# The exact rest of 30 weight slabs from an adding DMA in place of a VectorE subtraction

## The chip, the cores and the metric

The kernel runs on one core of a Trainium2 chip. The time is the device time of one execution in microseconds. Times are compared as medians over several runs.

## The reference

Two transformer-like blocks are applied to 512 tokens of width 1024 in float32. Every dense layer is a product of activations with a weight matrix of a size like 1024 x 5632 or 2816 x 1024.

```python
h = modulate(rmsnorm(x, norm1_g), shift1, scale1)        # shift, scale, gate: silu(c) @ ada_w + ada_b
u, v, val, gate = split(h @ w_in + b_in)                  # four parts of 512 columns
y_a = spatial_gating_mixer(gelu(u), gelu(v), ...)         # causal 128 x 128 mixing in chunks
y_b = conformer_conv_mixer(val, gate, ...)                # GLU, depthwise convolution of width 31, norm, silu
x = x + gate1 * (concat(rmsnorm(y_a), rmsnorm(y_b)) @ w_out)
g_ff, up_ff = split(modulate(rmsnorm(x, norm2_g), shift2, scale2) @ w_ffn_in)
x = x + gate2 * ((silu(g_ff) * up_ff) @ w_ffn_out)
...                                                       # then attention, pooling and two more FFNs
```

The change concerns the weights `w_in`, `w_out` and the first columns of `w_ffn_in`, all in the first block.

## The kernel before

TensorE multiplies in a rounded 32-bit type, float32r. To keep the accuracy of float32, each operand is split into a head and an exact rest: `wh` is the weight rounded to float32r, `wl` is the weight minus `wh`. An activation `H` is split in the same way into `hh` and `hl`. A product is then three matmuls, `wh*hh + wh*hl + wl*hh`. `Opd.mm3s` issues them in this order for each block k of 128 rows, into one PSUM accumulator, so `wl` of a slab is wanted by the third matmul of its group. `mm_tok` does the same with tokens as rows.

Weights come in slabs of 128 partitions x 1024 elements (0.5 MB). A slab of `w_in` for val, gate or u, or of `w_ffn_in`, has 8 blocks of 128 columns, which are runs of 512 bytes in memory; a slab for v has 2 blocks of 512 columns; a slab of `w_out` has 4 blocks of 256. The class `Weights` keeps a plan of all slabs in the order of their use (`plan`), loads one over SyncE's queue into a tile `raw` (`load`, line 309), and then `split` makes `wh` on ScalarE (a copy that rounds) and `wl` on VectorE (`raw - wh`). `W.look` says how many split slabs are to be ready ahead (4 here). The tiles `raw`, `wh`, `wl` and the tiles `adaw` of the conditioning weights share one pool of 37 buffers of 4 KB per partition, so a load can wait in SyncE's queue until a buffer comes free, and everything behind it in that queue waits too.

A scheduler at compile time sets the order of each engine's instructions and places the waits. In `split`, `tc.high_priority(offset=hp)` lets the slabs of `w_in` and `w_out` go ahead of other work (`HP` is 300 for them, 0 for the FFN). Up to line 828 the order on VectorE, ScalarE and TensorE is that of the program; after it the scheduler is free.

The order of the work around the change is this. The first four slabs (val and gate of c = 0 and 1) are multiplied while the conditioning is computed. Then come val and gate of c = 2 and 3 (four slabs), v (four), u (four), and the output projection `w_out` (eight). Between these products VectorE works off the depthwise convolution, one tap at a time (`tap`, `pump`). Of the taps of lag 17 or 23 and more (`ND`), ScalarE makes the scaled copy and GpSimd adds it (40 such additions on GpSimd). `ada_fetch` puts loads of `adaw` into the same SyncE queue. Then the first FFN starts: for each m a gate slab and an up slab, in two halves of 256 tokens for m = 0 to 2, and on all 512 tokens after that.

A flag `W.pool` could send a slab's subtraction to GpSimd. With `WP = 0` and `UP = 0` no slab is sent there.

Of the kernel before, what the change touches and what calls it, by code (L numbers as in the profile page):

```python
# [9 lines left out]
F32 = mybir.dt.float32  # L10
F32R = mybir.dt.float32r
AF = mybir.ActivationFunctionType
OP = mybir.AluOpType
# [7 lines left out]
FF = 2816  # L21
# [36 lines left out]
PP4 = 0  # L58
PP5 = 2
PP = (PP0, PP1, PP2, PP3, PP4, PP5)  # L60
WP = 0
UP = 0
PY = 4
PZ = 4
GNV = False
# [55 lines left out]
def body(ctx: ExitStack, tc: tile.TileContext, I: dict, out, dbg=None):  # L121
    nc = tc.nc
# [6 lines left out]
    V, G, SC, TE = (Ordered(tc, e) for e in (nc.vector, nc.gpsimd, nc.scalar, nc.tensor))  # L129
# [4 lines left out]
    def A(name, dt=F32):  # L134
        tag, bufs = TAGS.get(name, ("m", NB))
        return ar.tile([P, 2, S], dt, tag=tag, name=name, bufs=bufs)
# [22 lines left out]
    def act(o, i, f=AF.Identity, **kw):  # L159
        ins = SC.activation(o, i, f, **kw)  # L160
        if f in KEEPF and not SC.on:
            tc.keep_in_program_order(ins)
        return ins
# [120 lines left out]
    class Weights:  # L284


        def __init__(self, look):
            self.look, self.deep = look, 1
            self.specs, self.loaded, self.ready, self.done = [], [], [], 0
            self.pool = False  # L290
            self.hp = 0

        def plan(self, parts, kt, ncols):
            self.specs.append((parts, kt, ncols, self.pool, self.hp))

        def load(self):
            parts, kt, ncols, pool, hp = self.specs[self.done]
            n = kt * ncols

            def fl(t):  # L300
                return t.rearrange("p a c -> p (a c)")[:, :n]

            def v(t):
                return fl(t).rearrange("p (k m) -> p k m", k=kt)

            raw = ar.tile([P, 2, S], F32, tag="raw", name="raw", bufs=NR) if NR else A("raw")
            for (p0, p1, c0, c1, src, *ks) in parts:
                k0, k1 = ks or (0, kt)
                nc.sync.dma_start(v(raw)[p0:p1, k0:k1, c0:c1], src)
            self.done += 1  # L310

            def split():
                wh, wl = A("wh", F32R), A("wl", F32R)
                with tc.high_priority(offset=hp) if hp else nullcontext():
                    act(fl(wh), fl(raw), AF.Copy)
                    (G if pool else V).tensor_tensor(fl(wl), fl(raw), fl(wh).bitcast(F32), op=OP.subtract)
                self.ready.append((v(wh), v(wl), kt))
            self.loaded.append(split)

# [16 lines left out]
            return self.ready.pop(0)  # L336

    W = Weights(4)
    W.pool = True

    def rows_of(w, k0, kt, c0, n):
        return w[k0 * P:(k0 + kt) * P, c0:c0 + n].rearrange("(k p) m -> p k m", p=P)
# [1 line left out]
    def plan_cols(w, k0, kt, c0, n):  # L344
        W.plan([(0, P, 0, n, rows_of(w, k0, kt, c0, n))], kt, n)

    w_in = I["w_in"][0]
    for c in range(4):
        W.pool = c < WP
        W.hp = HP  # L350
        plan_cols(w_in, 0, 8, 1024 + c * P, P)
        plan_cols(w_in, 0, 8, 1536 + c * P, P)
# [5 lines left out]
        for g in range(4):  # L358
            plan_cols(I["w_out"][0], k0, 4, g * HS, HS)

    W.pool = False
    W.hp = 0

    def plan_ffn_tok(gate, up, down):
# [8 lines left out]
            for k0 in range(KT0, KF, 2):  # L373
                plan_cols(down, k0, 2, j * S, S)

    def plan_ffn(gate, up, down, pool=False):
        def gu(m):
            plan_cols(gate, 0, 8, m * P, P)
            plan_cols(up, 0, 8, m * P, P)

        def dn(m, k0, kts):
            for kt in kts:
                plan_cols(down, k0, kt, m * P, P)
                k0 += kt
        for m in range(KF0 + 1):
            W.pool = pool and m < 4
            gu(m)
        for m in range(KD - 1):
            dn(m, 0, (7, 7))
        for m in range(KF0 + 1, KF):  # L390
            gu(m)
        dn(KD - 1, 0, (7, 7))
        for m in range(KD):
            dn(m, KF0, (8,))

    plan_ffn(I["w_ffn_in"][0][:, :FF], I["w_ffn_in"][0][:, FF:], I["w_ffn_out"][0], UP)

    awi = I["attn_w_in_2"][0]
    FQ, FK, FV, FFG, NQ, KC, VC, KS, VS, KW, VW, NG = 0, 512, 1024, 1536, 1544, 2056, 2184, 2312, 2440, 2568, 2696, 2824
# [488 lines left out]
    for h in range(8):  # L888
        hp, e = divmod(h, 2)
# [399 lines left out]
    def K2(name):  # L1289
        return A(name, F32R), A(name, F32R)  # L1290
    ks, kw = K2("ks"), K2("kw")
# [489 lines left out]
```

## Time and profile before

| | |
|---|---|
| median of 3 runs | 1670.14 us (1670.02 to 1671.48) |
| profiled execution | 1667.07 us |
| its span, first to last instruction | 1665.3 us |
| TensorE busy | 1627.4 us |
| VectorE, ScalarE, GpSimd busy | 881.8, 681.8, 129.5 us |
| moved by DMA | 179.55 MB |
| mean granted clock of TensorE | 0.993 |

In the rows, PE is TensorE, DVE is VectorE, ACT is ScalarE, POOL is GpSimd, SPq is SyncE's queue. Most instructions bear the line of a helper, L113, so they are told apart by their tiles: `wl<-raw,wh` is the subtraction, `wh<-raw` the head. In a timeline a row can hold several like instructions (x2), and a bracket gives the engine's idle time before them and what ended it.

### The profile page before, as it was taken

What the parts mean: (1) busy time and instruction counts of PE and PEld (TensorE: products, weight loads), DVE (VectorE), ACT (ScalarE), POOL (GpSimd) and SP (SyncE); (2) the same over time, 40 slices, a digit from 0 to 9 for tenths busy, and PEclk for the clock granted to TensorE, in tenths of its full rate; (3) what the DMA queues carried; (4) which work ended last, traced back from release to release, by engine and by line L of the source; (5) the groups of instructions that cost most, each with busy time, mean ns of one, the idle gap of its engine ahead of it and who ended that gap; (6) DMA issues with size and microseconds to landing.
All of it is one profiled execution on the core that took longest, in us unless ns stands there. A gap on an engine that the chain in (4) does not pass through costs nothing.

```text
span 1665.3 us, 22096 instructions
## 1 busy us (share of the span) xinstructions
PE 1627.4 (98%) x8797; PEld 1358.9 (82%) x8797; DVE 881.8 (53%) x1645; ACT 681.8 (41%) x1232; POOL 129.5 (8%) x144
## 2 busy tenths in 40 slices
PE   7999899999999999999999999999999999999998
PEld 5776698887888998777778988888888998888886
DVE  5799585444333584678857344423257734432144
ACT  4585352222222364455658233213237823232232
POOL 0452000000000001100001000000013100000002
PEclk9999999999999999999999999999999999999999
DMA  9635435544531423311144232234134232232411
GB/s 306 179 111 193 152 112 175 154 149 133 153 101 54 120 57 90 90 26 52 39 107 124 61 111 61 95 114 144 59 102 114 77 89 77 83 121 93 121 64 51
DMA packets 245168, 179.55 MB, mean 108 GB/s; under 512 B 20688, under 2 KB 220224, under 8 KB 245064
## 3 DMA queue, kind: packets, MB, share of 16 engines
q1 hardware_dynamic: 240520, 176.99, 36.3%
q10 hardware_dynamic: 4544, 1.14, 0.4%
q8 instruction: 69, 1.13, 0.3%
q14 instruction: 35, 0.29, 0.1%
HBM read 175.99 MB, written 2.11 MB: 107 GB/s over the span
## 4 chain that ended last, share of the span: by engine, by line
PE 86%; DVE 3%; ACT 2%; issue 0%; DMA 0%; SPq 0%; DVEq 0%; ACTq 0%
PE mm L113 79%; PE ax L113 4%; PE st L113 3%; DVE pw L113 1%; ACT sq L113 0%; DMA raw<-in_w_out_dram 0%; ACT pw L113 0%; DVE XT L113 0%; DVE wl L113 0%; DVE sq L113 0%; ACT wh L113 0%; ACT H L113 0%; DVE pt L113 0%; DVE fk L113 0%; DVE mg L113 0%
## 5 line engine op out<-in xcount | busy, mean ns | idle before, releaser
L113 PE MATMUL mm<-H,wh 128*128 128x512 f32 (+1 forms) x3168 | 869.8, 361 | 9.2 <-ACT wh L113 3.4
L113 PEld LDWEIGHTS mm<-H,wh 128*128 128x128 f32 x3168 | 564.1, 189 | 104.5 <-issue 4.4
L113 PE MATMUL mm<-H,wl 128*128 128x512 f32 (+1 forms) x1584 | 567.7, 359 | 2.9 <-DVE wl L113 2.9
L113 DVE TENSOR_TENSOR wl<-raw,wh 128x1024 fp32r<-128x1024 f32 (+1 forms) x257 | 310.4, 1223 | 217.0 <-ACT wh L113 203.2
L113 PEld LDWEIGHTS mm<-H,wl 128*128 128x128 f32 x1584 | 299.3, 189 | 47.7 <-DVE wl L113 3.5
L113 ACT ACTIVATE wh<-raw 128x1024 fp32r<-128x1024 f32 (+1 forms) x257 | 262.5, 1041 | 127.3 <-PE mm L113 52.8
L113 PE MATMUL mm<-wh,hid 128*128 128x512 f32 x704 | 217.3, 389 | 0.0
L113 DVE TENSOR_TENSOR silu<-silu,mm 128x512 f32<-128x512 f32 (+1 forms) x77 | 47.0, 611 | 250.0 <-PE mm L113 243.5
L113 PEld LDWEIGHTS mm<-wh,hid 128*128 128x128 f32 x704 | 132.1, 188 | 27.1
L113 ACT ACTIVATE hid<-silu 128x512 fp32r<-128x512 f32 (+1 forms) x77 | 43.8, 569 | 242.5 <-DVE silu L113 234.9
L113 PE MATMUL mm<-wl,hid 128*128 128x512 f32 x352 | 137.3, 390 | 0.0
L113 PE MATMUL mm<-hid,wh 128*128 128x512 f32 (+1 forms) x464 | 116.4, 340 | 0.0
L113 PEld LDWEIGHTS mm<-hid,wh 128*128 128x128 f32 x464 | 80.3, 190 | 9.9 <-issue 0.4
L113 POOL TENSOR_TENSOR mg<-mg,gb 128x512 f32<-128x512 f32 x32 | 44.3, 1389 | 464.6 <-ACT sq L113 456.0
L113 ACT ACTIVATE silu<-silu 128x512 f32<-128x512 f32 (+1 forms) x52 | 29.3, 565 | 123.1 <-DVE silu L113 123.0
L113 PE MATMUL mm<-hid,wl 128*128 128x512 f32 (+1 forms) x232 | 79.1, 341 | 0.0
L113 PEld LDWEIGHTS mm<-wl,hid 128*128 128x128 f32 x352 | 66.1, 188 | 14.0 <-DVE wl L113 0.3
L113 DVE TENSOR_TENSOR silu<-mm,rsb 128x512 f32<-128x512 f32 (+1 forms) x52 | 31.6, 608 | 73.0 <-PE mm L113 72.5
L113 PE MATMUL mm<-wh,H 128*128 128x512 f32 (+2 forms) x256 | 67.0, 350 | 1.6 <-ACT wh L113 1.6
L113 DVE TENSOR_TENSOR hid<-silu,hid 128x512 fp32r<-128x512 f32 (+1 forms) x77 | 47.3, 614 | 37.4 <-ACT hid L113 37.3
L113 POOL TENSOR_TENSOR cv<-cv,tap 128x488 f32<-128x488 f32 (+12 forms) x40 | 52.5, 1348 | 88.2 <-ACT cv L113 71.2
L113 ACT ACTIVATE silu<-mm 128x512 f32<-128x512 f32 (+1 forms) x25 | 13.7, 546 | 108.7 <-PE mm L113 108.7
(271 smaller groups left out, 1624.7 us busy)
## 6 DMA issues: line engine op xcount, KB each, us to landing
adaw<-in_ada_w_dram SPq DMA_DIRECT2D x48, 512.0 KB
raw<-in_w_ffn_in_dram SPq DMA_DIRECT2D x44, 512.0 KB
raw<-in_ffn_w_gate_dram SPq DMA_DIRECT2D x44, 512.0 KB
raw<-in_ffn_w_up_dram SPq DMA_DIRECT2D x44, 512.0 KB
raw<-in_ffn_w_down_dram SPq DMA_DIRECT2D x44, 512.0 KB
raw<-in_w_in_dram SPq DMA_DIRECT2D x16, 512.0 KB
adaw<-in_ada_f_w_dram SPq DMA_DIRECT2D x16, 512.0 KB
raw<-in_attn_w_in_dram SPq DMA_DIRECT2D x16, 512.0 KB
```

Source lines behind the costliest of these rows:

```text
L113: ins = f(*a, **k)
```

## The change

A flag `dma` takes the place of `pool`. For a slab with the flag, ScalarE writes `-wh` into the tile `wl` (a second copy, with scale -1), and a DMA issued from GpSimd reads the weights once more from memory and adds them to that tile in SBUF: `wl = -wh + w`. VectorE does nothing for such a slab. Without the flag all stays as it was. The flag is set for val and gate of c = 2 and 3, and stays set for v, u and `w_out` (20 slabs); `UD = 5` sets it for gate and up of the first five m of the first FFN (10 slabs).

```diff
@@ -58,8 +58,7 @@
 PP4 = 0
 PP5 = 2
 PP = (PP0, PP1, PP2, PP3, PP4, PP5)
-WP = 0
-UP = 0
+UD = 5
 PY = 4
 PZ = 4
 GNV = False
@@ -287,14 +286,14 @@
         def __init__(self, look):
             self.look, self.deep = look, 1
             self.specs, self.loaded, self.ready, self.done = [], [], [], 0
-            self.pool = False
+            self.dma = False
             self.hp = 0
 
         def plan(self, parts, kt, ncols):
-            self.specs.append((parts, kt, ncols, self.pool, self.hp))
+            self.specs.append((parts, kt, ncols, self.dma, self.hp))
 
         def load(self):
-            parts, kt, ncols, pool, hp = self.specs[self.done]
+            parts, kt, ncols, dma, hp = self.specs[self.done]
             n = kt * ncols
 
             def fl(t):
@@ -313,7 +312,14 @@
                 wh, wl = A("wh", F32R), A("wl", F32R)
                 with tc.high_priority(offset=hp) if hp else nullcontext():
                     act(fl(wh), fl(raw), AF.Copy)
-                    (G if pool else V).tensor_tensor(fl(wl), fl(raw), fl(wh).bitcast(F32), op=OP.subtract)
+                    if dma:
+
+                        act(fl(wl), fl(wh).bitcast(F32), AF.Copy, scale=-1.0)
+                        for (p0, p1, c0, c1, src, *ks) in parts:
+                            k0, k1 = ks or (0, kt)
+                            nc.gpsimd.dma_start(v(wl)[p0:p1, k0:k1, c0:c1], src.bitcast(F32R), accum_op=OP.add)
+                    else:
+                        V.tensor_tensor(fl(wl), fl(raw), fl(wh).bitcast(F32), op=OP.subtract)
                 self.ready.append((v(wh), v(wl), kt))
             self.loaded.append(split)
 
@@ -336,7 +342,6 @@
             return self.ready.pop(0)
 
     W = Weights(4)
-    W.pool = True
 
     def rows_of(w, k0, kt, c0, n):
         return w[k0 * P:(k0 + kt) * P, c0:c0 + n].rearrange("(k p) m -> p k m", p=P)
@@ -346,7 +351,7 @@
 
     w_in = I["w_in"][0]
     for c in range(4):
-        W.pool = c < WP
+        W.dma = c >= 2
         W.hp = HP
         plan_cols(w_in, 0, 8, 1024 + c * P, P)
         plan_cols(w_in, 0, 8, 1536 + c * P, P)
@@ -358,7 +363,7 @@
         for g in range(4):
             plan_cols(I["w_out"][0], k0, 4, g * HS, HS)
 
-    W.pool = False
+    W.dma = False
     W.hp = 0
 
     def plan_ffn_tok(gate, up, down):
@@ -373,7 +378,7 @@
             for k0 in range(KT0, KF, 2):
                 plan_cols(down, k0, 2, j * S, S)
 
-    def plan_ffn(gate, up, down, pool=False):
+    def plan_ffn(gate, up, down, dma=0):
         def gu(m):
             plan_cols(gate, 0, 8, m * P, P)
             plan_cols(up, 0, 8, m * P, P)
@@ -383,7 +388,7 @@
                 plan_cols(down, k0, kt, m * P, P)
                 k0 += kt
         for m in range(KF0 + 1):
-            W.pool = pool and m < 4
+            W.dma = m < dma
             gu(m)
         for m in range(KD - 1):
             dn(m, 0, (7, 7))
@@ -393,7 +398,7 @@
         for m in range(KD):
             dn(m, KF0, (8,))
 
-    plan_ffn(I["w_ffn_in"][0][:, :FF], I["w_ffn_in"][0][:, FF:], I["w_ffn_out"][0], UP)
+    plan_ffn(I["w_ffn_in"][0][:, :FF], I["w_ffn_in"][0][:, FF:], I["w_ffn_out"][0], UD)
 
     awi = I["attn_w_in_2"][0]
     FQ, FK, FV, FFG, NQ, KC, VC, KS, VS, KW, VW, NG = 0, 512, 1024, 1536, 1544, 2056, 2184, 2312, 2440, 2568, 2696, 2824
```

## Rows read from the trace of the kernel before

**Rows 1.** The page of the profile: span, and busy time by engine.

```profile
span 1665.3 us, 22096 instructions
...
PE 1627.4 (98%) x8797; PEld 1358.9 (82%) x8797; DVE 881.8 (53%) x1645; ACT 681.8 (41%) x1232; POOL 129.5 (8%) x144
```

**Rows 2.** Stretches of 20 us: busy us by engine (count), TensorE clock, DMA share, GB/s.

```profile
60.00:80.00 20.00, 19.45 (x86) 15.82 (x85) 18.63 (x24) 13.41 (x19) 17.32 (x15) 1.00 0.82 236
80.00:100.00 20.00, 20.00 (x88) 16.18 (x88) 19.57 (x28) 11.68 (x19) 6.76 (x6) 1.00 0.00 1
100.00:120.00 20.00, 20.00 (x107) 15.52 (x106) 19.47 (x32) 18.00 (x31) 15.04 (x11) 1.00 0.42 135
120.00:140.00 20.00, 19.14 (x199) 14.06 (x197) 18.01 (x26) 18.50 (x27) 9.31 (x8) 1.00 0.89 324
...
200.00:220.00 20.00, 19.99 (x138) 18.77 (x137) 13.84 (x27) 8.60 (x16) 0.00 (x0) 0.94 0.14 39
```

**Rows 3.** Groups of instructions, 48 to 210 us: count, busy us, mean ns, idle before.

```profile
L113 DVE TENSOR_TENSOR wl<-raw,wh 128x1024 fp32r<-128x1024 f32 x20 | 26.5, 1325 | 5.4 <-ACT wh L113 5.3
L113 ACT ACTIVATE wh<-raw 128x1024 fp32r<-128x1024 f32 x21 | 22.0, 1048 | 7.1 <-DMA raw<-in_w_out_dram 3.0 <-DVE acc L113 2.3 <-DMA raw<-in_w_in_dram 1.7
```

**Rows 4.** TensorE's timeline, 55 to 80 us: start, us, instruction, count, idle before.

```profile
72.26 0.39 PE L113 MATMUL mm<-H,wl 128*128 128x512 f32 x1
...
79.76 0.50 PE L113 MATMUL mm<-wl,H 128*128 128x512 f32 x1 [0.55 <-DVE wl L113]
```

**Rows 5.** ScalarE's timeline, the wh copies of five slabs.

```profile
53.96 1.06 ACT L113 ACTIVATE wh<-raw 128x1024 fp32r<-128x1024 f32 x1 [0.57 <-DMA raw<-in_w_in_dram]
...
61.41 1.06 ACT L113 ACTIVATE wh<-raw 128x1024 fp32r<-128x1024 f32 x1 [1.11 <-DMA raw<-in_w_in_dram]
...
68.13 1.05 ACT L113 ACTIVATE wh<-raw 128x1024 fp32r<-128x1024 f32 x1
...
197.80 1.06 ACT L113 ACTIVATE wh<-raw 128x1024 fp32r<-128x1024 f32 x1 [3.05 <-DMA raw<-in_w_out_dram]
...
227.46 1.05 ACT L113 ACTIVATE wh<-raw 128x1024 fp32r<-128x1024 f32 x1
```

**Rows 6.** VectorE's timeline, two subtractions.

```profile
139.94 1.21 DVE L113 TENSOR_TENSOR wl<-raw,wh 128x1024 fp32r<-128x1024 f32 x1
...
198.89 1.23 DVE L113 TENSOR_TENSOR wl<-raw,wh 128x1024 fp32r<-128x1024 f32 x1 [2.74 <-ACT wh L113]
```

**Rows 7.** TensorE's timeline, the waits from 138 to 199 us.

```profile
140.07 0.51 PE L113 MATMUL mm<-H,wh 128*128 128x512 f32 x1 [0.80 <-DVE sp L113]
141.86 0.50 PE L113 MATMUL mm<-H,wh 128*128 128x512 f32 x1 [1.29 <-DVE H L113]
...
143.31 0.50 PE L113 MATMUL mm<-H,wh 128*128 128x512 f32 x1 [0.48 <-DVE H L113]
...
146.46 0.74 PE L113 MATMUL mm<-H,wh 128*128 128x512 f32 x2 [0.37 <-ACT H L113]
...
198.91 0.93 PE L113 MATMUL mm<-H,wh 128*128 128x256 f32 x3 [3.41 <-ACT wh L113]
```

**Rows 8.** SyncE's queue, four entries with their DMA issues.

```profile
49.79 0.38 SPq L309 DMA_DIRECT2D raw<-in_w_in_dram  x1
...
51.32 1.51 SPq L309 DMA_DIRECT2D raw<-in_w_in_dram  x1
...
178.36 12.42 SPq L636 DMA_DIRECT2D adaw<-in_ada_w_dram  x8
190.83 0.43 SPq L309 DMA_DIRECT2D raw<-in_w_out_dram  x1
```

**Rows 9.** GpSimd's timeline, the first run of convolution taps.

```profile
59.85 17.38 POOL L113 TENSOR_TENSOR cv<-cv,tap 128x488 f32<-128x488 f32 x13
```

**Rows 10.** What SyncE's queue waited for, 48 to 210 us: us, times, longest.

```profile
SPq L636 <- DVE X L113: 37.9, 1, 37.9
```

**Rows 11.** The chain that ended last, where the first FFN begins.

```profile
229.78 73.53 PE mm L113 x442
```

## Prediction

> **What bounds the kernel now.** The page of the profile comes first. TensorE is busy for 1627.4 us of the 1665.3 us span and VectorE, the engine that the change relieves, for 53% [rows 1]. So TensorE idles for 38 us in all, and only a part of that can be given back. The 30 slabs concerned are consumed before about 285 us, so the next view is the table of 20 us stretches [rows 2]. There the reader sees a VectorE that is full (18.0 to 19.6 of 20 us) between 60 and 140 us, and a TensorE that is full beside it. The two are near balance, and TensorE is the tighter one until 138 us.
>
> The timelines then say where TensorE really waited. There is 0.55 us at 79.76 us, on a `wl` [rows 4]. There are four short waits between 138 and 147 us, on VectorE's and ScalarE's operand `H` and `sp`, together 0.80 + 1.29 + 0.48 + 0.37 = 2.94 us [rows 7]. There is one wait of 3.41 us at 198.91 us, for a `wh` whose slab had just landed [rows 7]. That is nearly all that a relieved VectorE can repay in this part, 6.9 us or 0.4% of the time.
>
> **The change, part by part.** The flagged slabs are 4 (val and gate of c = 2, 3), 4 (v), 4 (u), 8 (`w_out`) and 10 (gate and up of the first five m).
>
> *Removed.* 20 subtractions of 1.325 us in the stretch 48 to 210 us are 26.5 us [rows 3]; the 10 of the FFN are at most 13 us more. On the path lies only what stands in front of the waits at 138 to 147 us: one `wl` of 1.21 us runs at 139.94 us among the `sp` and `H` steps [rows 6], and earlier ones pushed the whole queue back. The most that can come back is 2.94 + 0.55 = 3.5 us, the least nothing.
>
> *Added on ScalarE.* One more pass over the slab, like the `wh` copy of 1.05 us [rows 3]: 21 us by 210 us, 31 us in all. Between 100 and 140 us ScalarE has 18.0 + 18.5 of 40 us busy [rows 2], and four slabs fall there: 36.5 + 4.2 = 40.7 us. So ScalarE is about 0.7 us over and gives that back into the wait on `H`. I take 2.94 - 0.7 = 2.2 us as the gain at 138 to 147 us.
>
> *Added on the DMA engines.* Thirty more readings of 0.5 MB. Twelve of them, 6.3 MB, fall between 50 and 112 us; at the 236 GB/s of the stretch 60 to 80 us they take 27 us, and the stretches from 60 to 120 us leave 3.6 + 20 + 11.6 = 35 us of DMA time idle [rows 2]. So the engines have room, and the volume is costed at nothing. Without that cover the raw loads would be late, which is the upper bound below.
>
> *Moved: `wl` is complete later.* Before, `wl` follows `wh` by one instruction. Now it follows a second ScalarE pass (1.05 us), a turn on GpSimd's queue, and a transfer. No transfer that adds, and none issued by GpSimd, is in this trace. The nearest rows are the plain loads of the same slabs with the same 512-byte pieces. One issued at 49.79 us is used at 53.96 us by a `wh` that waited for it, 4.2 us. One issued at 51.32 us, which already took SyncE 1.51 us to issue, is used at 61.41 us by a `wh` that waited for it, 10.1 us. One at 190.83 us is used at 197.80 us, 7.0 us [rows 5, 8]. Below 4.2 us I see no reason to go, since reading, adding and writing is not less work. I take 5.0 us, near the lower row because few loads are in flight when most of these start, and keep 4.2 and 10.1 us as ends.
>
> GpSimd's queue is in order too: from 59.85 us it runs 13 convolution taps without a gap, 1.34 us each [rows 9]. A transfer issued there waits 0.7 us on average, and the taps behind it wait for its slab. The taps on GpSimd run beside VectorE's own taps of the same channels, and only the sum of both is used, so their delay is costed at nothing. Where GpSimd becomes the later of the two, it is the third rival.
>
> Where is 1.05 + 5.0 us too late? The rest of a slab is wanted by the third matmul of its group, so there is no grace after `wh`.
> - *Gate of c = 3.* `wh` starts at 68.13 us [rows 5]; 68.13 + 1.05 + 1.05 + 0.7 + 5.0 = 75.9 us. TensorE wants it at 72.26 us [rows 4]. It is late by 3.7 us. The v slabs after it come out late by less than that, and TensorE, full from there to 138 us [rows 2], cannot catch up. Ends: 2.9 and 8.8 us.
> - *The seventh `w_out` slab.* Here the chain is load, `wh`, `wl`, TensorE, with nothing to hide behind. `wh` starts at 197.80 us [rows 5], and the subtraction ended at 198.89 + 1.23 = 200.1 us [rows 6]. New: 197.80 + 1.05 + 1.05 + 5.0 = 204.9 us, 4.8 us later. Ends: 4.0 and 9.9 us. The load itself is late because SyncE's queue holds it behind eight `adaw` loads that start at 178.36 us [rows 8].
> - *FFN slabs.* TensorE begins them at 229.78 us [rows 11] and spends 2 x 48 short matmuls of 0.12 us on m = 0 and 1, so m = 2 is wanted after 241 us. Its gate slab has `wh` at 227.46 us [rows 5] and so its rest at 227.46 + 2.1 + 5.0 = 234.6 us: 6 us of cover, and the earlier ones have more. Costed at nothing up to a transfer of 11 us; without the cover each would cost what the `w_out` slab does, 4.8 us.
>
> *Raw buffers.* They come free after `wh` instead of after the subtraction, some 2 us earlier, which can start a load sooner. I cost it at nothing in the sum, since the two late slabs were held by other things; it is a rival below.
>
> **Sum.** 3.7 - 2.2 + 4.8 = +6.3 us. The profiled execution took 1667.07 us around its span of 1665.3 us, 3.1 us under the median of 1670.14 us, so 1673.4 us for it and 1676.4 us for the median. Ends: 2.9 + 4.0 - 3.5 = +3.4 us (1673.5) and 8.8 + 9.9 - 0 = +18.7 us (1688.8). What a measurement here can tell from no change is 0.2%, 3.3 us.
>
> **Rivals.**
> *Faster.* The loads start earlier. SyncE's eight `adaw` loads before the seventh `w_out` slab waited 37.9 us for a VectorE instruction [rows 10]; with 26.5 us of work taken off VectorE and raw buffers released by ScalarE, that wait may end earlier. It decides when the slab lands 5 us or more before 197.8 us. Then the 3.41 us go, with them the 2.94 us, and the clock's fall after that pause (0.94 granted from 200 to 220 us, so a part of it at the lower of TensorE's two levels [rows 2], 1.2 us). That is -7.6 us, and with half of the 3.7 us still lost, about -5.5 us: 1664.6 us. For it: the wait names VectorE. Against it: the instruction named (`X`) itself hangs on TensorE's products.
>
> *No change.* The late slab at 68.13 us waited for no load, only its turn on ScalarE [rows 5]. If the compiled order puts it some 2 us earlier, and the transfer is at its lower end, 2.9 - 2 = 0.9 us are left there, 4.0 at 198 us, and with 3.5 us repaid the sum is +1.4 us: 1671.5 us. The Trainium skill (DMA: Bandwidth & Descriptors, Anatomy of one DMA) gives a transfer issued by GpSimd about 2.0 us plus its bytes at 436 GB/s, which for a slab would be 3.2 us, an estimate from that page; by it the sum would be 1.9 - 2.2 + 3.0 = +2.7 us. The nearest row, 4.2 us for a plain load, lies above it.
>
> *GpSimd becomes the bound: much slower.* From 60 to 120 us its taps take 39.1 us [rows 2]. If issuing one transfer holds the engine for g, twelve of them fit only up to g = (62 - 39) / 12 = 1.9 us. SyncE's issue of a load takes 0.38 us [rows 8], a GpSimd pass over 488 elements 1.34 us [rows 9]. At g = 3 us the queue is 13 us behind by 112 us, and TensorE with it: +6.3 + 13 = 1689 us or more. The same skill (GPSIMD Engine Reference, When to use GPSIMD) has two of the engine's own cores write the descriptors of such a transfer, which speaks for a g above SyncE's; no run here shows it yet.
>
> **How the numbers follow.** The forecast (1673.5 to 1688.8) gets 0.37: every link of it is a row, and the unknown transfer can hardly be faster than a load. Faster gets 0.32, because three of TensorE's waits are there to be repaid and the order of the loads can shift. No change gets 0.23, GpSimd as the bound 0.08. So slower by over 0.2% has 0.45, within 0.2% 0.23, faster 0.32. The range for all cases runs from 1662 to 1690 us: it takes in the faster case at -8 us and the upper end of the forecast, and leaves out about half of the heavy case and little else.
>
> **What would show it.** The trace after should show 30 GpSimd issues and 30 more ScalarE passes of 1.05 us, 30 subtractions fewer on VectorE, and the time from a second pass's end to the first matmul that uses it. A wait of some 4 us on a transfer near 72 us and one of about 8 us near 199 us would bear out the sum; no waits near 140 us, the gain. The prediction is wrong if transfers land within 3 us, if the seventh `w_out` slab is loaded earlier, or if GpSimd's issues are long and its queue is full from 60 to 140 us.

## The result, and the profile of the kernel after

The changed kernel takes 1696.95 us (median of 6 runs, 1694.04 to 1699.26), the kernel before 1670.0 us beside it. The ratio is 1.016, with a 95% interval of 1.0149 to 1.0171: 27 us slower. The sign was forecast, 1676.4 us was not, and the time lies above the range that was given (1662 to 1690 us).

The page of the profile after gives span, busy time by engine and, for the DMA queues, packets, megabytes and their share of 16 engines' span:

```profile
span 1695.2 us, 22217 instructions
...
PE 1634.8 (96%) x8797; PEld 1363.5 (80%) x8797; DVE 848.5 (50%) x1615; ACT 711.4 (42%) x1263; POOL 166.6 (10%) x174
...
q1 hardware_dynamic: 240520, 176.99, 35.8%
q0 software_dynamic: 24032, 15.73, 6.9%
```

Beside [rows 1], VectorE gave up 33.3 us and ScalarE took on 29.6 us, as forecast. TensorE runs the same 8797 matmuls. The span is 29.9 us longer: TensorE's idle time grew by 22.5 us (60.4 against 37.9) and its busy time by 7.4 us, for the same work at a mean granted clock of 0.985 against 0.993. The last two lines are new: q1 carries the loads, q0 the 30 transfers. A load's packets take 0.358 x 1695.2 / 176.99 = 3.4 us of all 16 engines per megabyte, an adding transfer's 0.069 x 1695.2 / 15.73 = 7.4 us, 2.2 times as much.

The stretches of 20 us, with the columns of [rows 2]:

```profile
60.00:80.00 20.00, 15.34 (x52) 12.08 (x53) 7.21 (x12) 5.90 (x9) 8.90 (x8) 0.77 1.07 232
80.00:100.00 20.00, 15.83 (x68) 12.19 (x66) 15.97 (x25) 14.69 (x20) 12.98 (x11) 1.00 0.82 156
...
140.00:160.00 20.00, 12.83 (x121) 10.44 (x120) 4.94 (x8) 16.59 (x22) 6.48 (x7) 0.95 0.52 148
160.00:180.00 20.00, 16.92 (x120) 9.49 (x120) 15.06 (x18) 17.61 (x26) 10.88 (x9) 0.80 0.98 245
```

From 60 to 80 us every engine is idle much of the time, VectorE most (7.21 of 20 us, 18.63 before). Only the DMA's share is higher than before (1.07 against 0.82), and it moves no more (232 GB/s against 236). TensorE waits, and its granted clock falls to 0.77: part of the stretch runs at the lower of its two levels.

The view of what TensorE waited for in the first 400 us (total, times, longest), and its timeline at three of those waits:

```profile
PE mm L112 <- DMA wl<-in_w_in_dram: 14.2, 4, 6.3
...
PE mm L112 <- ACT uT L112: 4.5, 1, 4.5
PE mm L112 <- ACT vt L112: 4.0, 1, 4.0
PE mm L112 <- ACT sq L112: 3.1, 1, 3.1
```

```profile
61.99 0.80 PE L112 MATMUL mm<-H,wl 128*128 128x512 f32 x1 [6.32 <-DMA wl<-in_w_in_dram]
72.13 0.47 PE L112 MATMUL mm<-H,wl 128*128 128x512 f32 x1 [2.68 <-DMA wl<-in_w_in_dram]
...
87.56 0.47 PE L112 MATMUL mm<-H,wl 128*128 128x512 f32 x1 [2.69 <-DMA wl<-in_w_in_dram]
```

The waits answer to [rows 4, 7]. The first is for the rest of val of c = 2, which the prediction did not go through at all. It named only the gate of c = 3, the last of the four slabs, whose rest makes TensorE wait at 87.56 us. How that slab fared is seen on ScalarE's timeline, and on GpSimd's, where the transfers are issued:

```profile
64.19 1.06 ACT L112 ACTIVATE wh<-raw 128x1024 fp32r<-128x1024 f32 x1 [0.32 <-DMA raw<-in_w_in_dram]
...
79.02 0.69 ACT L112 ACTIVATE sg<-mm,fixed 128x512 f32<-128x512 f32 x1 [13.78 <-PE mm L112]
79.61 1.05 ACT L112 ACTIVATE wl<-wh 128x1024 fp32r<-128x1024 f32 x1
```

```profile
63.62 2.21 POOL L320 DMA_DIRECT2D wl<-in_w_in_dram  x1
...
80.96 1.56 POOL L320 DMA_DIRECT2D wl<-in_w_in_dram  x1 [12.05 <-ACT wl L112]
```

Its head starts 4 us sooner than before, at 64.19 us instead of 68.13 [rows 5]. But the second pass stands behind `sg`, an evacuation that waits 13.78 us for the product of gate of c = 2, and that product had waited for its own transfer (at 72.13 us). The first three transfers go out at 51.67, 56.96 and 63.62 us; the fourth hangs on the second: transfer, product, evacuation, second pass, transfer.

Last, the time from issue to landing of the transfers up to 330 us, which is the prediction's 5.0 us:

```profile
DMA to landing us min/median/max: 5.8/6.9/15.0
```

### The profile page after: what moved, and what is told of

It reads as the page before. It is cut to its first block, busy times and chain, and to the rows that moved or that the text cites. A ratio compares the mean times of both kernels' runs of the same rounds, so it can differ in the third digit from the quotient of the medians.

```text
span 1695.2 us, 22217 instructions
## 1 busy us (share of the span) xinstructions
PE 1634.8 (96%) x8797; PEld 1363.5 (80%) x8797; DVE 848.5 (50%) x1615; ACT 711.4 (42%) x1263; POOL 166.6 (10%) x174
## 3 DMA queue, kind: packets, MB, share of 16 engines
q1 hardware_dynamic: 240520, 176.99, 35.8%
q0 software_dynamic: 24032, 15.73, 6.9%
## 4 chain that ended last, share of the span: by engine, by line
PE 88%; DVE 5%; DMA 3%; ACT 3%; issue 1%; POOL 0%; SPq 0%; DVEq 0%; ACTq 0%; POOLq 0%
PE mm L112 81%; PE ax L112 4%; PE st L112 3%; DMA wl<-in_w_in_dram 1%; DVE pw L112 1%; DMA raw<-in_w_ffn_in_dram 1%; ACT sq L112 1%; ACT wh L112 0%; DVE wl L112 0%; DMA xtok<-in_x_dram 0%; DVE ax L112 0%; ACT pw L112 0%; DVE H L112 0%; DVE uT L112 0%; ACT wl L112 0%
## 5 line engine op out<-in xcount | busy, mean ns | idle before, releaser
L112 DVE TENSOR_TENSOR wl<-raw,wh 128x1024 fp32r<-128x1024 f32 (+2 forms) x227 | 271.1, 1211 | 208.7 <-ACT wh L112 195.9
```

The source lines that it names most:

```text
L112: ins = f(*a, **k)
```

## The experiments

Ratios are to the kernel before, run beside each, with a 95% interval. All edits but one control start from the changed kernel. Three theories stand against each other. **A**: each product waits for its own chain of head, second pass, issue and transfer. **B**: the adding transfers fill the DMA engines and hold everything up. **C**: ScalarE has no room for the second pass.

**Where: four parts of the change alone.**

```diff
e1  -        W.dma = c >= 2
    +        W.dma = False                 # FFN's ten slabs only
e2  UD = 0; W.dma = False after the loop over c   # val and gate of c = 2, 3 only
e3  UD = 0; flag only for v and u
e4  UD = 0; flag only for w_out
```

> Only the ten slabs of the FFN's first five row groups get their rest by the adding transfer; the twenty slabs of the first stage are subtracted on VectorE as before. The late-handover theory (A: a product waits for a transfer that lands 6 to 15 us after its issue, wherever the slab is wanted at once): these slabs are wanted 6 us or more after their split, so no loss, 1669 to 1672. The volume theory (B: an adding transfer holds the DMA engines about 2.2 times as long per byte as a load, and pushes the loads back): a third of the 27 us, 1679. The ScalarE theory (C: the second pass of about 1.05 us): ScalarE is not full from 260 us on, so 1670 to 1673.

> Only the four value and gate slabs of c = 2 and 3 get the adding transfer. A: these are the slabs that are wanted at once; the v products began 16 us later in the changed kernel, so 1680 to 1687. B: 4 of 30 transfers, 1672 to 1674. C: four passes of 0.6 to 1.05 us, in a stretch where ScalarE is 30 to 70 per cent busy, 1671 to 1674.

> Only the eight slabs of v and u get the adding transfer. A: v's slabs are split some us ahead of their product, u's further ahead, so a small loss, 1670 to 1676. B: 8 of 30, in the fullest stretch of the DMA (60 to 120 us), 1675 to 1680. C: eight passes where ScalarE is 70 to 90 per cent busy, up to 8 us, 1674 to 1678.

> Only the eight slabs of the out-projection get the adding transfer. A: the 7th slab's rest was worked out as 4.8 us late, 1672 to 1676. B: 8 of 30 at 140 to 230 us, where the raw slabs load late too, 1674 to 1680. C: eight passes of 1.05 us between 140 and 180 us, where ScalarE is over 80 per cent busy and the product waits for its evacuations: up to 8 us, 1675 to 1680.

| part | slabs | time, us | ratio | predicted, us |
|---|---|---|---|---|
| e1 FFN | 10 | 1680.6 | 1.0067 (1.0050 to 1.0084) | 0 |
| e2 val, gate | 4 | 1678.2 | 1.0051 (1.0035 to 1.0067) | +3.7 |
| e3 v, u | 8 | 1674.0 | 1.0027 (1.0014 to 1.0039) | 0 |
| e4 `w_out` | 8 | 1682.1 | 1.0074 (1.0059 to 1.0089) | +4.8 |

Every part costs. The parts add up to 2.2%, more than the whole (1.6%); that a wait which is there already hides some of the next is a reading. No theory foretold all four: B came near for e1 and A held for e3, but e2 and e4 lie outside every range that was given for them. The FFN's slabs, costed at nothing, cost 0.67%. In e1 one sees its gate slab of m = 2 go out from GpSimd and TensorE take it:

```profile
235.82 1.55 POOL L320 DMA_DIRECT2D wl<-in_w_ffn_in_dram  x1 [5.83 <-ACT wl L112]
...
245.65 0.55 PE L112 MATMUL mm<-H,wl 128*128 128x256 f32 x1 [4.16 <-DMA wl<-in_w_ffn_in_dram]
```

The prediction had its rest there at 234.6 us; it came at 245.5. The cover of 6 us went in two ways: the head was made at 231.83 us instead of 227.46 (raw slabs landed late: one `wh` before it waited 2.17 us for its load), and the transfer took 9.7 us. TensorE's wait of 4.16 us is not all of the 11 us that e1 lost: from 200 to 260 us its granted clock was 0.89 to 0.91, where it had been 0.94 to 1.00.

**The seventh and eighth slab of `w_out`.** The flag stands only for these two.

```diff
             for g in range(4):
+                W.dma = k0 == 4 and g >= 2
```

> Only the last two slabs of the out-projection (the 7th and 8th, whose raw slabs are loaded last, after 190 us) get the adding transfer. The prediction's term for the 7th slab was 4.8 us. If all of the out-projection's loss of 12 us is here: 1681 to 1683. By the prediction's term: 1674 to 1676. By a loss that comes from the first six slabs at 130 to 160 us: 1669 to 1672.

1676.96 us, 1.0052 (1.0035 to 1.0069): 70% of what all eight cost. ScalarE, GpSimd and TensorE at the seventh slab:

```profile
199.11 1.04 ACT L112 ACTIVATE wl<-wh 128x1024 fp32r<-128x1024 f32 x1
...
200.47 1.47 POOL L320 DMA_DIRECT2D wl<-in_w_out_dram  x1 [56.69 <-DMA raw<-in_w_ffn_in_dram]
...
208.80 0.58 PE L112 MATMUL mm<-H,wl 128*128 128x256 f32 x1 [5.64 <-DMA wl<-in_w_out_dram]
```

This is the prediction's chain, link by link. Only the transfer is longer, 208.80 - 200.47 = 8.3 us. The rest is there at 208.8 us instead of 200.1 [rows 6], 8.7 us later. The ratio makes 8.7 us of 1668.6 us, too, but its interval is 5.8 to 11.5 us: the agreement to the tenth is chance. TensorE's own wait is 5.64 us, since it had other matmuls to do first, and its granted clock from 200 to 220 us was 0.71, where it had been 0.94 [rows 2].

**ScalarE's second pass alone, and the pass on VectorE.** In e5 VectorE adds the slab from SBUF to the negative head, and there is no transfer. In e6 VectorE writes the negative head and the transfer adds as before. e17 is e6 for the four slabs of e2 only.

```diff
e5  -   nc.gpsimd.dma_start(v(wl)[...], src.bitcast(F32R), accum_op=OP.add)
    +   V.tensor_tensor(fl(wl), fl(raw), fl(wl).bitcast(F32), op=OP.add)
e6  -   act(fl(wl), fl(wh).bitcast(F32), AF.Copy, scale=-1.0)
    +   ts(fl(wl), fl(wh).bitcast(F32), -1.0, OP.mult)
```

> The thirty slabs keep ScalarE's second pass (the rest's tile gets minus the head) but VectorE adds the slab from SBUF; there is no second reading and no transfer on GpSimd's queue. A: the wait for the transfer is gone, and only the second pass is left in the chain: 1671 to 1678. B: no second reading, so 1670 to 1674. C: ScalarE does what it does in the changed kernel, so most of the loss stays: 1685 to 1697.

> The negative head is written by VectorE (a multiplication by minus one) instead of ScalarE; the transfer adds as in the changed kernel. A: the transfer's delay stays, less what the second pass stood behind ScalarE's evacuation: 1682 to 1692. B: the volume is the same, 1693 to 1697. C: ScalarE is as free as before, so 1672 to 1680.

> Only the four value and gate slabs of c = 2 and 3, as in the run that took 1678, but VectorE writes the negative head. In that run the fourth slab's second pass began 15 us after its head, behind an evacuation on ScalarE that waited for the product before it. If this order on ScalarE makes the loss of the four slabs: 1670 to 1674. If the transfers' own time does (9 and 14 us from issue to use for the first two): 1675 to 1680.

e5: 1669.2 us, 1.0001 (0.9992 to 1.0011). On balance thirty passes more on ScalarE cost nothing, so C falls as the cause of the loss. It is a balance, though. Of the waits that the changed kernel has for ScalarE, e5 has the longest one, too, without any transfer (the view of TensorE's waits in e5, 30 to 400 us):

```profile
PE mm L112 <- ACT uT L112: 4.5, 1, 4.5
...
PE mm L112 <- DVE H L112: 2.7, 1, 2.7
```

From 130 to 160 us TensorE's waits in e5 add up to 9.8 us, where the kernel before had 2.94 [rows 7]; a part comes back because its last two `w_out` loads go out at 185.68 us instead of 190.83 [rows 8] and the 3.41 us at 198.91 us are gone.

e6: 1697.8 us, 1.0175 (1.0160 to 1.0190): with all thirty slabs it changes little which engine makes the negative head. e17: 1674.3 us, 1.0034 (1.0022 to 1.0047), against 1.0051 for e2. The fourth transfer goes out at 73.52 us instead of 81.36 us:

```profile
73.52 1.55 POOL L320 DMA_DIRECT2D wl<-in_w_in_dram  x1 [1.10 <-issue]
```

So the order on ScalarE makes about a third of the four slabs' loss, though the two intervals overlap at 1.0035 to 1.0047; the rest is left to the transfers' own time (8.4 to 14.9 us there).

**The chain and the addition, one at a time.** e7 leaves the order as it is, but the transfer overwrites. e11 overwrites and takes the second pass away, so that nothing has to be made before the transfer. e13 is e11 with the addition, to a tile that was set to zero.

```diff
e7  -   nc.gpsimd.dma_start(..., accum_op=OP.add)
    +   nc.gpsimd.dma_start(...)
e11     as e7, and
    -   act(fl(wl), fl(wh).bitcast(F32), AF.Copy, scale=-1.0)
e13 -   act(fl(wl), fl(wh).bitcast(F32), AF.Copy, scale=-1.0)
    +   V.memset(fl(wl).bitcast(F32), 0.0)
```

> As the changed kernel, but the transfer overwrites the rest's tile with the slab and adds nothing (the product is then that of the head plus the slab). The same volume, order and waits, only no addition. If the addition in the DMA is what is slow (A and B by its price per byte): 1678 to 1688. If it is the handover of any second transfer, or ScalarE (C): 1692 to 1697.

> GpSimd's transfer overwrites the rest's tile with the slab, without addition, and nothing writes the tile before it, so it waits for no pass of ScalarE and can run beside the load of the raw slab (the product is then that of the head plus the slab). The run that overwrites after ScalarE's second pass took 1686. If the step from ScalarE to GpSimd, after the head is made, is what the products wait for: 1670 to 1677. If it is the volume in the queues: 1683 to 1687.

> The transfers add as in the changed kernel, but to a tile that VectorE has set to zero ahead of time, not to minus the head; so a transfer waits neither for the raw slab nor for ScalarE (the product is then that of the head plus the slab). Against the run of the same order that overwrites (1670) it prices the addition; against the changed kernel (1697) it prices the wait behind raw load, head and second pass. If that chain of waits makes the loss: 1668 to 1674. If the adding itself (its double time on the DMA engines, GpSimd's longer issue) makes the 11 us that the overwriting transfer in the changed kernel's order did not have: 1679 to 1683.

| | overwrites | adds |
|---|---|---|
| waits for no head | e11: 1.0008 (0.9993 to 1.0023) | e13: 1.0088 (1.0073 to 1.0103) |
| waits for head and second pass | e7: 1.0102 (1.0085 to 1.0119) | change: 1.0160 (1.0149 to 1.0171) |

This table separates the two. Reading the thirty slabs a second time costs nothing on balance, if nothing has to come before the transfer: e11 waits 3.6 us for transfers, and its last two `w_out` loads go out at 167.47 us, so that the 3.41 us at 198.91 us are gone. The chain costs 0.7 to 0.9%, adding 0.6 to 0.8%, and together they make the 1.6%. The chain's price takes in the order on ScalarE: e7 has waits of 4.02 and 3.89 us for `vt` and `uT`, e13 of 0.95 and 3.56 us (without a second pass), e11 has none. e7 (1686.2 us) lies in the range given for the addition, e11 (1669.8) at the end of that for the step from ScalarE, and e13 (1684.7) just above its second range. The price of adding is seen in the queue's line and the stretch 60 to 80 us of e11 and e13:

```profile
q0 software_dynamic: 24032, 15.73, 5.5%
...
60.00:80.00 20.00, 16.69 (x67) 13.29 (x66) 16.35 (x25) 12.42 (x18) 18.14 (x18) 0.91 1.25 303
```

```profile
q0 software_dynamic: 24032, 15.73, 6.7%
...
60.00:80.00 20.00, 13.45 (x51) 10.70 (x52) 11.94 (x18) 8.16 (x13) 13.10 (x12) 0.77 1.25 248
```

At the same share of the engines, 1.25, the overwriting kernel moves 303 GB/s and the adding one 248. Such a share is not a measure of how full the engines are: it adds up the time of packets and can pass 1, as in e11 from 180 to 200 us, where TensorE is busy for 18.91 of 20 us (15.59 before):

```profile
180.00:200.00 20.00, 18.91 (x168) 16.33 (x156) 7.11 (x16) 8.81 (x12) 6.76 (x8) 1.00 1.75 289
```

By the queue's line e11's packets take 0.055 x 1667.4 / 15.73 = 5.8 us per megabyte, e7's 5.3, e13's 7.2. So overwriting the rest's float32r tile already takes 1.5 to 1.7 times a load's 3.4 us, and adding takes 1.2 to 1.4 times as long as overwriting.

A landing takes 7.3 us in e11 (median) and 10.3 us in e13; e11's longer landings cost nothing, because they start at 42 us and lie beside the raw loads. In e13 the first transfer goes out only at 53 us, behind VectorE's zeroing (30 passes, 27.4 us), so a part of its 0.88% is that start.

**Half the bytes.** Each transfer adds only the first half of its slab's blocks.

```diff
-   nc.gpsimd.dma_start(v(wl)[p0:p1, k0:k1, c0:c1], src.bitcast(F32R), accum_op=OP.add)
+   kh = (k0 + k1) // 2
+   nc.gpsimd.dma_start(v(wl)[p0:p1, k0:kh, c0:c1], src.bitcast(F32R)[:, :kh - k0], accum_op=OP.add)
```

> As the changed kernel, but each transfer adds only the first half of its slab's row blocks; the other half of the rest stays minus the head, so the result is not the reference's. If the loss is made by bytes (time of a transfer and load on the engines, A and B alike): half of the 27 us, 1681 to 1685. If it is a fixed cost of each handover (issue, start, order behind other work): 1690 to 1697.

1683.0 us, 1.0095 (1.0068 to 1.0121): 0.65% less than the whole. The landing takes 4.9 us (median) instead of 6.9. Half the bytes take 41% of the loss away, 24 to 58% by the interval of e10. Taken as linear, some 80% of the loss goes with the bytes; the interval leaves room for half of it as a fixed price of each handover.

**Volume without a reader.** VectorE subtracts as before, and the transfers bring the same slabs somewhere else: e8 adds them to two scratch tiles, e9 to the raw tile after its last use, e16 overwrites that raw tile.

```diff
     V.tensor_tensor(fl(wl), fl(raw), fl(wh).bitcast(F32), op=OP.subtract)
+    if dma:
e8      act(fl(sc)[:, :1], fl(wh).bitcast(F32)[:, :1], AF.Copy); nc.gpsimd.dma_start(v(sc)[...], src, accum_op=OP.add)
e9      nc.gpsimd.dma_start(v(raw)[...], src, accum_op=OP.add)
e16     nc.gpsimd.dma_start(v(raw)[...], src)
```

> The rest is subtracted on VectorE as before, and the same thirty slabs are also added by GpSimd's transfers into two scratch tiles that nobody reads; each transfer waits for a one-column ScalarE copy from the slab's head, and for the transfer two before it. Only the volume and GpSimd's issues are left of the change. B: most of the loss stays, 1685 to 1695. A and C: 1670 to 1676. If GpSimd's issues delay the taps (the rival of GpSimd as the bound): 1675 to 1685, with the wait at the taps' end.

> The rest is subtracted on VectorE as before; after the subtraction the same thirty slabs are added by GpSimd's transfers into the raw tile, which nobody reads any more. Volume, price per byte and GpSimd's issues are those of the changed kernel; no product waits for a transfer, and no engine but GpSimd waits for one (the scratch tiles of the run before made ScalarE and GpSimd wait for transfers; here only the raw tile's buffer comes free later). A (the product waits for its own transfer): 1670 to 1674. B (volume): 1678 to 1684, as with the scratch tiles.

> As the run in which the subtraction stays on VectorE and the thirty slabs are added to the raw tile that nobody reads any more (1686), but the transfer overwrites the raw tile with the same slab. Same bytes, same waits of GpSimd for VectorE, no addition. If adding is what loads the DMA engines and delays the loads and GpSimd: 1671 to 1676. If it is that GpSimd waits for VectorE and so runs its taps later, in one piece, against VectorE's subtractions: 1681 to 1687.

1680.4 us, 1.0069 (1.0054 to 1.0084); 1685.9 us, 1.0115 (1.0083 to 1.0146); 1679.0 us, 1.0059 (1.0040 to 1.0078). By these, volume alone would cost 10 to 19 us. e8 falls into the range given for GpSimd's issues delaying the taps; e9 and e16 fall into none of theirs. But they do not price the volume, because they lose time in another place, on VectorE. TensorE's longest wait in e9 in that part is for the end of the convolution (its waits from 30 to 400 us):

```profile
PE st L112 <- DVE cv L112: 7.0, 1, 7.0
```

VectorE's subtractions in e9, 48 to 210 us (count, busy us, mean ns), and both engines' timelines at one of them:

```profile
L112 DVE TENSOR_TENSOR wl<-raw,wh 128x1024 fp32r<-128x1024 f32 x18 | 38.7, 2149 | 1.4 <-ACT wh L112 1.4
```

```profile
62.74 6.29 DVE L112 TENSOR_TENSOR wl<-raw,wh 128x1024 fp32r<-128x1024 f32 x1
```

```profile
61.66 6.28 POOL L112 TENSOR_TENSOR cv<-cv,tap 128x488 f32<-128x488 f32 x5
```

The mean was 1325 ns [rows 3]. While GpSimd works off five taps in one piece, a subtraction that takes 1.2 us elsewhere lasts 6.29 us, and ends 1.1 us after the fifth. Thirteen taps in a row were there before, too [rows 9]; they took 1.34 us each, these 1.26 us, and the three subtractions that began beside them took 2.08, 1.56 and 1.38 us:

```profile
62.51 2.08 DVE L113 TENSOR_TENSOR wl<-raw,wh 128x1024 fp32r<-128x1024 f32 x1 [0.67 <-ACT wh L113]
```

So a row of taps alone does not do it. My reading, which no run here tests, is that the taps pile up behind GpSimd's waits for VectorE and its issues, and then leave no gap between them. In e8, ScalarE and GpSimd wait for the scratch tiles as well. So the price of the addition rests on e7, e11 and e13; e9 against e16, with like waits on VectorE in both, makes 0.56% of it. Their queue lines (e9 first) show the addition into a tile that is plain float32:

```profile
q0 software_dynamic: 24032, 15.73, 7.0%
```

```profile
q0 software_dynamic: 4320, 15.73, 3.1%
```

That is 7.5 us per megabyte for adding and 3.3 us, with fewer packets, for overwriting, which is what a load takes.

**Splitting further ahead.** Six split slabs ahead instead of four, in the changed kernel (e14) and in the kernel before (e15).

```diff
-    W = Weights(4)
+    W = Weights(6)
```

> The changed kernel, but slabs are split up to six products ahead instead of four, so that each transfer is issued earlier before its product. If the loss is the transfer's time between split and product, much of it is hidden: 1675 to 1688. If it is volume on the DMA engines, or the raw loads arrive too late to be split earlier: 1692 to 1699.

> The control of the run before: the kernel before the change with six products ahead. No wait for a transfer is there to be hidden: 1668 to 1673 by every theory, unless the earlier loads crowd others out.

e14: 1701.5 us, 1.0188 (1.0171 to 1.0205). It lies above both ranges that were expected. It does not put the chain to the test, because the transfers hardly go out sooner: the twelve of `w_in` from 52.57 to 124.82 us (51.67 to 127.66 us in the changed kernel), the first of the FFN at 233.19 us instead of 227.56. e15: 1665.0 us, 0.9966 (0.9955 to 0.9978), faster than both kernels and than expected. Its queue on SyncE loads the last two slabs of `w_out` at 163 us instead of 191 us [rows 8]:

```profile
163.34 1.40 SPq L309 DMA_DIRECT2D raw<-in_w_out_dram  x2
```

With that the wait of 3.41 us at 198.91 us [rows 7] is gone, and the order of the loads gives what relief of VectorE does not.

## Why the prediction was right in sign and wrong in size

The step that failed is the search for late slabs ("Where is 1.05 + 5.0 us too late?"). It followed three places, found two late slabs of thirty, worth 3.7 and 4.8 us, and put the rest at nothing. Measured one by one, every group is late: 8.5 us for val and gate, 4.5 for v and u, 12.4 for `w_out`, 11.2 for the FFN; 27 us together. That a rest comes late because its transfer follows a second pass was right, and so was the sign.

- *Transfer, 5.0 us with 4.2 and 10.1 as ends.* Too small. Landings took 5.8 us at least, 6.9 in the median and up to 15.0. At the seventh `w_out` slab, with the flag on the last two slabs alone (e12), it was 8.3 us, which makes +8.7 us of +4.8. By the fit that the prediction quoted from the Trainium skill (DMA: Bandwidth & Descriptors, Anatomy of one DMA) it would have been an estimated 3.2 us; no adding landing here came near that, and the measurement decides.
- *Volume, "costed at nothing".* Right on balance for bytes that no product has to wait for (e11: 1.0008), wrong for adding, which makes 0.6 to 0.8%. The sum priced a byte like a load's; the packets of an adding transfer take 2.2 times as long. By that the 6.3 MB of the first twelve transfers would take an estimated 6.3 x 7.4 = 47 us of all engines, where 35 us were idle. But e11's, at 5.8 us, would take 37 us and lost nothing, so that full engines are the cause is not shown.
- *Gate of c = 3, +3.7 us.* The place was right, the chain was not. The first of the four slabs already made TensorE wait (6.32 us), and the second pass did not follow the head but stood 15 us behind it. The four slabs cost 0.51%.
- *FFN slabs, nothing.* Wrong: 0.67%. The cover of 6 us was real but was used up by later raw slabs and a transfer of 9.7 us. The prediction gave the condition itself (a transfer of up to 11 us), but not the lateness of the loads.
- *v and u, not costed.* 0.27%.
- *Relief at 138 to 147 us, -2.2 us.* It did not come back. VectorE stands idle there (4.94 of 20 us busy), and TensorE waits 4.0 and 4.5 us for ScalarE's `vt` and `uT`. ScalarE works without a pause from 150.43 to 162.08 us, two second passes among its work (2.1 us); the rest is work that the scheduler put in front of `vt` and `uT`. The term took ScalarE to be 0.7 us over; e5 shows that its load is free only on balance.
- *Rivals.* "GpSimd as the bound" fell: an issue takes 1.20 to 1.59 us in 27 of 30 rows and 2.21 at most, where 1.9 us was the limit worked out, and though its taps ran later too, VectorE waited only 0.3 us for them from 40 to 200 us. "Faster by earlier loads" did not come: the seventh `w_out` load went out at 203.40 us instead of 190.83. Its mechanism is real where no chain holds the loads back: 185.68 us in e5, 167.47 in e11.

What stays open: why packets that overwrite a float32r tile take 1.5 to 1.7 times as long as a load's and adding ones 2.2 times, and how much of each run's difference is the order of the instructions, which the scheduler chose anew for every kernel.

## What to carry to other kernels

A transfer that ends a chain (load, head, second pass, issue, transfer, product) is priced by its landing under the load of that stretch, not by the quiet landings of plain loads, and every slab of the group is followed, not the latest alone. An adding transfer is charged by the time of its own packets, here 2.2 times a load's. And relief of an engine is worth no more than the waits that name it: here 0.55 + 0.80 + 1.29 + 0.48 = 3.1 us for VectorE, not the 6.9 us of all waits, and two slabs more of lookahead gave 0.34% of the time without any transfer.

## What the hardware showed that was not expected

VectorE's passes stretch while GpSimd works through a row of its own instructions: the subtraction from 1.2 to 6.29 us in e9, and in e17 the multiplication by minus one, which has one input and takes 0.69 us elsewhere. Both engines' timelines there:

```profile
61.65 4.44 DVE L112 TENSOR_SCALAR wl<-wh 128x1024 fp32r<-128x1024 f32 x1
```

```profile
61.50 4.03 POOL L112 TENSOR_TENSOR cv<-cv,tap 128x487 f32<-128x487 f32 x3
```

The Trainium skill (SBUF — State Buffer, Who interferes with whom) says that VectorE and GpSimd share a pair of ports and that the one that starts second waits for the other's whole instruction. The rows agree with the sharing; but 4.44 and 6.29 us are as long as three and five taps, so here VectorE's instruction lasted through several in a row, not one. Beside the thirteen taps of the kernel before it lasted 2.08 us at most; what makes the difference is open.

The granted clock fell after some waits of a few microseconds: in the stretch in which TensorE waited 6.32 and 2.68 us it was 0.77, in that with the wait of 4.50 us 0.80, while in that with the single wait of 2.69 us it stayed at 1.00. Of the 29.9 us that the span grew, 7.4 us are the same matmuls, some of them at the lower of the two levels.
